# Down-projection weight sums of a fast matrix product moved to a DRAM scratch, twelve fast blocks for ten, and the first loads reordered

## The chip, the cores and the metric

The kernel runs on one core of a Trainium2 chip. Five engines work side by side, each on its own list of instructions in order: TensorE (PE, matrix products; PEld is its weight load), VectorE (DVE), ScalarE (ACT), GpSimd (POOL) and SyncE (SP). Transfers are issued by SP, ACT or POOL and carried out by 16 DMA engines. What counts is the device time of one execution in microseconds (us). The kernel before takes 942.4 us, the median of three runs between 942.28 and 942.5.

## The reference

Two layers of a decoder over 256 tokens of 1024 features, all in float32:

```python
for l in range(DEPTH):                       # 2
    u = rms_norm(h, norm_mix_pre[l])
    proj = u @ w_in[l]                       # q, k, v, xr, yr, pp, gates
    attn_br = sliding_window_attention(q, k, v, sinks) @ w_attn_br[l]
    hr = rg_lru(causal_depthwise_conv(xr, ...), ...)
    rnn_br = (hr * gelu(yr)) @ w_rnn_br[l]
    pool_br = multi_scale_pool(pp, ...) @ w_pool_br[l]
    merged = g0 * attn_br + g1 * rnn_br + g2 * pool_br      # g = sigmoid(gates)
    h = h + rms_norm(merged @ w_out[l], norm_mix_post[l])
    m = rms_norm(h, norm_mlp_pre[l])
    y = square(relu(m @ w_mlp_up[l])) @ w_mlp_down[l]       # 1024 -> 4096 -> 1024
    h = h + rms_norm(y, norm_mlp_post[l])
```

## The kernel before, in words

**Weights.** Every weight matrix is cut into units of 128 x 1024 floats (512 KB). A unit is loaded by SP into one of seven buffers `raw` (`load_to`, L163), split into a high and a low part by ACT (L95) and DVE (L96) (`split_to`; eight buffers `wh`, eight `wl`), and used by TensorE. A full product takes three matmuls, high x high, high x low, low x high (`mm3`, L103 to L105). A load waits until DVE has split the unit that held its buffer seven loads earlier. `take(n)` hands out the next n units and splits as far as needed; `ahead` splits two more.

**A layer** runs in stages: key/value and query projections (12 units); the branch stage, a list `ORDER` of 26 steps (`pp0 gp0 pp1 ... br1`, 74 units), with the attention's parts spread between them; the output projection (8 units); the MLP. Steps with `pp`, `yr`, `xr` take a pair of units (`w_unit2`, L336 and L338) and end in `joined` (L344, L345); steps with `g` are gates (`gate`, L743) and steps with `b` projections (`project`), four units each.

**The MLP.** The 4096 hidden features are 16 blocks of 256. `up(j)` makes block j (two units, 48 matmuls of 256 columns). Ten blocks (`nstr = NBLK - PLAIN`) then go through a Strassen product: `down(j)` makes seven products of three matmuls of 512 columns, 21 in all. The last six (`PLAIN`) go through `plain`: two halves of the block, two of the tokens, two of the columns, three matmuls each, 24 in all. `UPS` says how many `up` run in the step of each Strassen block. The seven products need the block's two down units in four forms `w1` to `w4`. `w1` is the first unit and `w4` half of the second. `w2` and `w3` are sums of quarters of the two: `dma_sums` makes the 1024 columns of `w2` for two blocks at a time with POOL transfers into SBUF, a plain load (L870) and an adding one (L872); `weight_sums` adds the two halves of `w3` on DVE (L887, L888); `weight_forms` splits both. After the Strassen blocks `drain` combines four of the products on DVE while the plain blocks run; the last three plain blocks (`LAST`) are done token tile by token tile.

**The start.** `x` comes in two tiles of 128 tokens: the first half of tile 0 first, its second half between the two halves of weight unit 0, tile 1 after unit 1. `first_features` transposes a quarter of `x` on TensorE (L245) and writes it scaled as high and low part (L249, L250). `warm_up` (L136) runs idle matmuls between. `KV_ORDER` is the order in which the four units of the first projection meet the two token tiles.

**Order.** A scheduler puts each engine's instructions in order at build time; POOL and SP carry them out one after the other, each waiting for what it needs. POOL does, before the change, the small zero fills of `joined`'s buffers (L604, L702) and the twenty loading and adding transfers of each layer's sums.

Of the kernel before, what the change touches and what calls it, by code (L numbers as in the profile page):

```python
# [26 lines left out]
WARM = (6, 2, 2)  # L27
# [4 lines left out]
X1_AT = 2  # L32
# [6 lines left out]
PLAIN = 6  # L39
LAST = 3  # L40

UPS = (2, 1, 1, 2, 1, 1, 2, 1, 1, 1)
NBLK = 16
SQRT_2_PI = 0.7978845608028654
# [9 lines left out]
KV_ORDER = ((0, 0), (1, 0), (0, 1), (1, 1), (2, 0), (2, 1), (3, 0), (3, 1))  # L54
KV_MID = 1
# [8 lines left out]
def trunk(ctx, tc, x, wts, rgw, par, gpost, eye, ctab, out):  # L64
# [11 lines left out]
    psum = ctx.enter_context(tc.tile_pool(name="psum", bufs=8, space=PSUM))  # L76

# [56 lines left out]
    def warm_up(n):  # L134
        for i in range(n):
# [3 lines left out]
    NHU = wts.shape[0]  # L139
    st = {"load": 0, "split": 0, "use": 0}  # L140
    raw_t, hu_t = {}, {}

    nstr = NBLK - PLAIN
    pair_at = [[(l + 1) * (NHU // L) - 64 + 6 + 2 * j + 2 * (sum(UPS[:j - 1]) + 1 if j else 0) for j in range(nstr)]
               for l in range(L)]
    half = {i + 1 for at in pair_at for i in at}

    per_layer = NHU // L
    fine = {i + l * per_layer for l in range(L) for i in [*range(FINE[0]), *range(per_layer - 64, per_layer - 64 + FINE[1])]}

    def load_to(n):
        while st["load"] < min(n, NHU):
            i = st["load"]
            r = raws.tile([P, HU_COLS], F32, tag="raw", name=f"raw{i}")
            if i == 0:
                for k in range(2):
                    nc.sync.dma_start(r[:, 512 * k:512 * k + 512], wts[i][:, 512 * k:512 * k + 512])
                    if k == 0:
                        nc.sync.dma_start(h[:, 0, 512:1024], x[0:P, 512:1024])
            elif i in half:  # L160
                nc.sync.dma_start(r[:, 512:1024], wts[i][:, 512:1024])
            else:
                nc.sync.dma_start(r[:], wts[i])  # L163
            raw_t[i] = r
            st["load"] += 1

    def split_to(n):
        while st["split"] < min(n, NHU):
# [3 lines left out]
            wh = his.tile([P, HU_COLS], F32R, tag="wh", name=f"wh{i}")  # L172
            wl = los.tile([P, HU_COLS], F32R, tag="wl", name=f"wl{i}")
            parts = 2 if i in fine else 1
            for k in range(parts):
                sl = slice(k * HU_COLS // parts, (k + 1) * HU_COLS // parts)
                split(wh[:, sl], wl[:, sl], r[:, sl])
# [10 lines left out]
    def ahead():  # L188
        split_to(st["use"] + AHEAD)
# [152 lines left out]
    def joined(o, pss, first):  # L342
        for n, ps in enumerate(pss):
# [78 lines left out]
    load_to(X1_AT)  # L422
    nc.sync.dma_start(h[:, 1, :], x[P:T, :])
    fa, fb = first_features(0, 0), first_features(0, 1)
# [4 lines left out]
    next(fb)  # L429
    warm_up(WARM[2])  # L430
    next(fb)
    split_to(2)
# [3 lines left out]
    for l in range(L):  # L436
# [14 lines left out]
        def kv_first():  # L451

            pss = [bank([P, 512]) for _ in range(2)]
            for n, (i, tt) in enumerate(KV_ORDER):
# [4 lines left out]
                if n == KV_MID:  # L459
                    for part in range(2):  # L460
                        for _ in hp(first_features)(1, part):
                            pass
# [105 lines left out]
        if l == 0:  # L568
# [3 lines left out]
            hq = take(4)  # L572
            q0 = [qkv_part(1, tt, hq) for tt in range(2)]
# [25 lines left out]
        def unit_pp(j):  # L599
# [4 lines left out]
            nc.gpsimd.memset(xp[:, :, 0:16], 0.0)  # L604
# [88 lines left out]
        def unit_xr(j):  # L693
            rg = ttile([P, 2, 2, P], nm="rg")
            nc.sync.dma_start(rg[:], rgw[l, j])
# [6 lines left out]
            nc.gpsimd.memset(xp[:, :, 0:3], 0.0)  # L702
# [37 lines left out]
        def gate(br, nh):  # L740
            for tt, ps in enumerate(t_unit(uh, ul, nh)):
                th = ttile([P, 512], nm="th")
                A.activation(th[:], ps[:], AF.Tanh, scale=0.5 if l else nrm[:, tt, 2:3])  # L743
                ths[br, nh, tt] = th
            ahead()
# [15 lines left out]
        for nm in ORDER:  # L761
            kind, j = nm[0:2], int(nm[2])
            if nm == "pg0":
# [46 lines left out]
        prods, t8s = {}, {}  # L810
# [28 lines left out]
        def up(j):  # L839
            ps = w_unit(take(2), uh, ul)  # L840
# [23 lines left out]
        def dma_sums(j0):  # L864


# [281 lines left out]
```

## Time and profile before

| | us |
|---|---|
| median of 3 runs | 942.4 |
| profiled execution | 942.54 |
| its span, first to last instruction | 940.8 |
| PE busy / DVE / ACT / POOL | 932.4 / 757.2 / 631.8 / 37.7 |
| DMA bytes | 188.98 MB, mean 201 GB/s |
| of these issued by POOL | 20.97 MB |

"Busy" of PE counts a matmul from its start to its modelled end, so matmuls that follow each other closely overlap, and the spacing of the starts is what a matmul costs. The chain of waits goes back from the last instruction, each time to what released it. The DMA share of a stretch is the mean busy time of the 16 DMA engines; it counts the time that packets took, waiting for memory included. In layer 0 the branch stage lies between 44 and 272 us and the MLP between 290 and 460; in layer 1 some 463 us later.

### The profile page before, as it was taken

Reading aid. Unit: us, or ns where it says so; the run is one execution under the profiler, and the core shown is the slowest. Engines: PE = TensorE matmul, PEld = TensorE weight load, DVE = VectorE, ACT = ScalarE, POOL = GpSimd, SP = SyncE. Lnnn points to the kernel's source line nnn. Section 1 sums busy time; section 2 is a strip of 40 time slices with the busy share of each in tenths; the row PEclk is TensorE's granted clock in tenths of the full one; section 3 lists DMA queues with packets and bytes.
Section 4 is the critical chain, followed back from the end, with each engine's and each line's share of the span. In section 5 each row is a group of like instructions: output and inputs, shape, how many; then the busy total and the mean of one; then the engine's idle time right before and its main releaser. Section 6 shows DMA issues by size and latency. Waiting matters only on the chain.

```text
span 940.8 us, 14349 instructions
## 1 busy us (share of the span) xinstructions
PE 932.4 (99%) x5196; PEld 801.2 (85%) x5196; DVE 757.2 (80%) x1365; ACT 631.8 (67%) x1092; POOL 37.7 (4%) x60
## 2 busy tenths in 40 slices
PE   9999999999999999999999999999999999999997
PEld 6888987888888999998888888888888889999986
DVE  6878997889868887988586788786898598888964
ACT  7765765689637786767475666656896468767741
POOL 0000000000011111100000000000000110110000
PEclk9999999999999999999999999999999999999999
DMA  8855454643867888957457545545438688987631
GB/s 333 289 198 163 152 188 137 218 150 117 283 208 200 254 245 264 271 169 253 134 190 258 170 148 178 179 141 189 161 109 299 176 266 233 264 255 236 219 95 45
DMA packets 57351, 188.98 MB, mean 201 GB/s; under 512 B 6080, under 2 KB 6720, under 8 KB 57280
## 3 DMA queue, kind: packets, MB, share of 16 engines
q1 hardware_dynamic: 48528, 166.79, 53.0%
q0 software_dynamic: 8320, 20.97, 9.9%
q8 instruction: 41, 0.67, 0.3%
q10 hardware_dynamic: 432, 0.30, 0.1%
q14 instruction: 30, 0.25, 0.1%
HBM read 186.99 MB, written 1.05 MB: 200 GB/s over the span
## 4 chain that ended last, share of the span: by engine, by line
PE 99%; DMA 0%; DVE 0%; ACT 0%; SPq 0%; DVEq 0%; issue 0%
PE ps L103 18%; PE ps L104 18%; PE ps L105 18%; PE ps L336 9%; PE ps L376 8%; PE pr L103 6%; PE pr L104 6%; PE pr L105 6%; PE ps L338 5%; PE ps L507 1%; PE ps L555 1%; PE ps L544 1%; PE ps L259 1%; PE ps L487 0%; DMA h<-x 0%; PE ps L736 0%
## 5 line engine op out<-in xcount | busy, mean ns | idle before, releaser
L96 DVE TENSOR_TENSOR wl<-raw,wh 128x1024 fp32r<-128x1024 f32 (+1 forms) x304 | 334.2, 1123 | 69.2 <-ACT wh L95 60.8
L95 ACT ACTIVATE wh<-raw 128x1024 fp32r<-128x1024 f32 (+1 forms) x304 | 288.3, 983 | 138.7 <-PE ps L105 52.8
L103 PE MATMUL ps<-m,wh 128*128 128x256 f32 x448 | 126.8, 283 | 0.0
L105 PE MATMUL ps<-m,wl 128*128 128x256 f32 x448 | 126.8, 283 | 0.0
L104 PE MATMUL ps<-m,wh 128*128 128x256 f32 x448 | 126.7, 283 | 0.0
L336 PE MATMUL ps<-u,wh 128*128 128x512 f32 x384 | 96.9, 394 | 0.0
L103 PEld LDWEIGHTS ps<-m,wh 128*128 128x128 f32 x448 | 85.9, 192 | 1.0
L104 PEld LDWEIGHTS ps<-m,wh 128*128 128x128 f32 x448 | 85.9, 192 | 1.0
L105 PEld LDWEIGHTS ps<-m,wl 128*128 128x128 f32 x448 | 85.9, 192 | 0.0
L103 PE MATMUL ps<-wh,u 128*128 128x512 f32 x208 | 82.4, 396 | 0.0
L104 PE MATMUL ps<-wl,u 128*128 128x512 f32 x208 | 81.6, 392 | 0.0
L105 PE MATMUL ps<-wh,u 128*128 128x512 f32 x208 | 81.1, 392 | 0.0
L336 PEld LDWEIGHTS ps<-u,wh 128*128 128x128 f32 x384 | 69.4, 189 | 13.6 <-issue 0.7
L338 PEld LDWEIGHTS ps<-u,wl 128*128 128x128 f32 x384 | 52.4, 190 | 3.8
L338 PE MATMUL ps<-u,wl 128*128 128x256 f32 x384 | 53.5, 282 | 0.0
L103 PEld LDWEIGHTS ps<-wh,u 128*128 128x128 f32 x208 | 39.4, 190 | 9.0 <-issue 0.7
L105 PEld LDWEIGHTS ps<-wh,u 128*128 128x128 f32 x208 | 39.3, 189 | 8.4
L104 PEld LDWEIGHTS ps<-wl,u 128*128 128x128 f32 x208 | 39.3, 189 | 7.8 <-DVE wl L96 0.3
L526 ACT ACTIVATE pr<-ps,s 128x128 f32<-128x128 f32 (+1 forms) x64 | 25.9, 430 | 20.1 <-DVE s L517 15.7
L376 PE MATMUL ps<-wh,u 128*128 128x512 f32 x160 | 38.6, 392 | 0.0
L104 PE MATMUL pr<-wl,hid 128*128 128x512 f32 (+1 forms) x102 | 38.5, 378 | 0.0
L103 PE MATMUL pr<-wh,hid 128*128 128x512 f32 (+1 forms) x102 | 38.4, 377 | 0.0
(262 smaller groups left out, 1996.5 us busy)
## 6 DMA issues: line engine op xcount, KB each, us to landing
raw<-wts SPq DMA_DIRECT2D x295, 512.0 KB, 4.5
dsum<-wts POOLq DMA_DIRECT2D x40, 512.0 KB, 6.6
raw<-wts SPq DMA_DIRECT2D x22, 256.0 KB, 4.6
gB<-gpost SPq DMA_DIRECT2D x4, 512.0 KB, 7.5
rg<-rgw SPq DMA_DIRECT2D x8, 256.0 KB, 4.2
out<-h SPq DMA_DIRECT2D x3, 256.0 KB, 2.0
h<-x SPq DMA_DIRECT2D x2, 256.0 KB, 3.7
h<-x SPq DMA_DIRECT2D x1, 512.0 KB, 6.5
```

Of the source, the lines that this page charges most:

```text
L95: A.activation(hi, src, AF.Copy)
L96: V.tensor_tensor(out=lo, in0=src, in1=hi.bitcast(F32), op=ALU.subtract)
L103: PE.matmul(o, lh, rh, start=start, stop=False, **kw)
L104: PE.matmul(o, lh, rl, start=False, stop=False, **kw)
L105: PE.matmul(o, ll, rh, start=False, stop=stop, **kw)
L259: PE.transpose(banks[c // 4][:, c % 4, :], src[c // 4][:, (c % 4) * P:(c % 4 + 1) * P], ident)
L336: PE.matmul(ps[:], ws[0][c], x2[:, :, c, :], start=c == 0, stop=False)
L338: PE.matmul(ps[:, 0, :], ws[1][c], x2[:, 0, c, :], start=False, stop=c == 7)
L376: PE.matmul(o, xx[:, c, tsl], ww[c], start=(n == 0 and c == 0), stop=(n == 2 and c == 7))
L507: PE.matmul(sc[hd // hp][:, hd % hp, :], qT[a, j // 2][rows, j % 2, blk * P:(blk + 1) * P], kTs[0][rows, a, 0:w], start=True, stop=True)
L526: A.activation(pr[:, j, :], sc[i][:, j, :], AF.Exp, bias=negm[:, hd:hd + 1], accum_out=sums[:, hd:hd + 1])
L544: PE.transpose(ps[:, g, :], g8["p"](4 * b + g)[:, kt * P:(kt + 1) * P], ident)
```

## The change

The four forms of a Strassen block's weights are now all loaded as stream units. `w1` and `w4` come from a new input `dnw` that holds the pairs; `w2` and `w3` come from a scratch tensor in DRAM, one of 1 MB for each block and layer, which transfers alone fill during the branch stage. For the twelve steps 2, 4, ... 24 of `ORDER` one block is made, in six transfers:

1. POOL writes a few bytes of a tile that the branch stage has just made (`mark`) into the scratch. What fills the scratch must wait for this.
2. SP copies two times 512 KB from `dnw` into the scratch, DRAM to DRAM.
3. POOL issues three adding transfers one after the other, DRAM to DRAM: 512 KB, 256 KB, 256 KB; each needs what was there before.

`PLAIN` goes from 6 to 4, so twelve blocks of a layer are Strassen blocks and four are plain. `dma_sums`, `weight_sums` and `weight_forms` go. The zero fills go from POOL to DVE. The recurrence's small weights `rg` are loaded two steps of `ORDER` ahead. At the start `x` is loaded in quarters among the first weight units, the key/value projection takes both token tiles of a unit before the next unit, and the first query projection follows unit by unit in the same way (`q_first`).

```diff
-WARM = (6, 2, 2)
+WARM = (6, 3)
+X_AFTER = {0: ((1, 0),), 1: ((0, 1), (1, 1))}
-PLAIN = 6
+PLAIN = 4
-UPS = (2, 1, 1, 2, 1, 1, 2, 1, 1, 1)
+UPS = (2, 1, 1, 1, 1, 1, 1, 1, 1, 1, 1, 1)
+BATCH, SUM_AT = 1, tuple(range(2, 26, 2))
-KV_ORDER = ((0, 0), (1, 0), (0, 1), (1, 1), (2, 0), (2, 1), (3, 0), (3, 1))
+KV_ORDER = ((0, 0), (0, 1), (1, 0), (1, 1), (2, 0), (2, 1), (3, 0), (3, 1))
...
+    def sums_copy(l, j0):
+        t = sums[l, j0]
+        nc.gpsimd.dma_start(t[:, :, 0, 0:1].rearrange("b i n -> (b i) n"), mark["t"])
+        for k in range(BATCH):
+            nc.sync.dma_start(t[k, 0], dnw[l, j0 + k, 0])
+            nc.sync.dma_start(t[k, 1].rearrange("p (b n) -> p b n", b=2),
+                              dnw[l, j0 + k, :, :, 512:1024].rearrange("b p n -> p b n"))
+    def sums_add(l, j0, step):
+        t = sums[l, j0]
+        for k in range(BATCH):
+            if step == 0:
+                dst = t[k, 0].rearrange("p (b n) -> p b n", b=2)
+                src = dnw[l, j0 + k, 1, :, 0:512].unsqueeze(1).to_broadcast([P, 2, 512])
+            elif step == 1:
+                dst, src = t[k, 1, :, 0:512], t[k, 0, :, 0:512]
+            else:
+                dst, src = t[k, 1, :, 512:1024], t[k, 1, :, 0:512]
+            nc.gpsimd.dma_start(dst, src, accum_op=ALU.add)
...
+        def pair(j):
+            stream.extend([(dnw[l, j, 0], HU_COLS), (dnw[l, j, 1, :, 512:1024], 512)])
+        def sum_units(j):
+            stream.extend((sums[l, j // BATCH * BATCH][j % BATCH, i], HU_COLS) for i in range(2))
...
+        def q_first():
+            pss = [bank([P, 512]) for _ in range(2)]
+            for i in range(4):
+                hu, = take(1)
+                for tt in range(2):
+                    s_hu(pss[tt][:], hu, uh, ul, 2 * i, tt, i == 0, i == 3)
+                ahead()
+            return [qkv_out(1, tt, pss[tt]) for tt in range(2)]
...
-            nc.gpsimd.memset(xp[:, :, 0:16], 0.0)
+            V.memset(xp[:, :, 0:16], 0.0)
...
-        for nm in ORDER:
+        rgs_raw = {}
+        for k, nm in enumerate(ORDER):
             kind, j = nm[0:2], int(nm[2])
+            for nm2 in ORDER[k:k + 3]:
+                if nm2[0:2] == "xr" and int(nm2[2]) not in rgs_raw:
+                    rgs_raw[int(nm2[2])] = rg = ttile([P, 2, 2, P], nm="rg")
+                    nc.sync.dma_start(rg[:], rgw[l, int(nm2[2])])
+            if k in SUM_AT:
+                j0 = BATCH * SUM_AT.index(k)
+                sums_copy(l, j0)
+                for step in range(3):
+                    sums_add(l, j0, step)
...
-        def dma_sums(j0):
-            t = acts.tile([P, 2, 2, 512], F32, tag="lo", name="dsum")
-            for j in js:
-                nc.gpsimd.dma_start(t[:, j - j0], wts[pair_at[l][j]].rearrange("p (b n) -> p b n", b=2))
-            for j in js:
-                nc.gpsimd.dma_start(t[:, j - j0], wts[pair_at[l][j] + 1][:, 0:512].unsqueeze(1).to_broadcast([P, 2, 512]),
-                                    accum_op=ALU.add)
...
-            V.tensor_tensor(out=t34[:, 0, :], in0=t12[:, 0, :], in1=r0[:, 512:1024], op=ALU.add)
-            V.tensor_tensor(out=t34[:, 1, :], in0=t34[:, 0, :], in1=r1[:, 512:1024], op=ALU.add)
```

The names of the scratch tensors in the lists below are `sums0_9` for block 9 of layer 0; a load `raw78` is the stream unit with number 78, counted from 0. What the change moves in the lists of instructions, at the three places of which the prediction speaks:

SP's list in the branch stage of layer 0, around the load of unit 78, the first of the projection `br0`; before:

```order
L163 DMA raw76_2461<-wts 128x1024 [waits DVE_49]
L163 DMA raw77_2525<-wts 128x1024 [waits DMAHW1_49,DVE_49]
L163 DMA raw78_2545<-wts 128x1024 [waits DMAHW2_49,DVE_49,Activation_49]
L163 DMA raw79_2563<-wts 128x1024 [waits DMAHW3_49,DVE_49,Activation_49]
L163 DMA raw80_2581<-wts 128x1024 [waits DMAHW4_49,DMAHW5_49,DVE_49,Activation_49]
```

and with the change:

```order
L215 DMA raw76_2547<-wts 128x1024 [waits DMAHW3_49,DVE_49,Activation_49]
L215 DMA raw77_2611<-wts 128x1024 [waits DMAHW4_49,DVE_49]
L155 DMA sums0_9_115<-dnw 16x8192 [waits DMAHW5_49,DMASW4_49]
L156 DMA sums0_9_115<-dnw 256x1x512 [waits DMAHW6_49]
L155 DMA sums0_10_116<-dnw 16x8192 [waits DMAHW7_49,DMASW5_49]
L156 DMA sums0_10_116<-dnw 256x1x512 [waits DMAHW0_49]
L215 DMA raw78_2637<-wts 128x1024 [waits DMAHW1_49,DVE_49,Activation_49]
L215 DMA raw79_2655<-wts 128x1024 [waits DMAHW2_49,DVE_49,Activation_49]
```

Four copies into the scratch now stand between the loads of units 77 and 78, and the first of each pair waits for one of POOL's transfers (DMASW), the mark of its block.

POOL's list before, from the branch stage of layer 0 to the first sums of the MLP:

```order
L604 MEMSET xp 128x2x16 x4
L702 MEMSET xr 128x2x3 x4
L870 DMA dsum<-wts 128x1024 x2
L872 DMA dsum<-wts 128x2x512 x2
L870 DMA dsum<-wts 128x1024 x2
```

and with the change, from the marks of blocks 9 and 10 to that of block 11:

```order
L153 DMA sums0_9_115<-xr_2349 2x1 [waits DVE_49]
L153 DMA sums0_10_116<-xr_2349 2x1
L169 DMA sums0_9_115<-dnw 256x1x512 [waits DMAHW5_49,DMASW4_49]
L169 DMA sums0_10_116<-dnw 256x1x512 [waits DMAHW7_49,DMASW7_49,DMASW5_49]
L169 DMA sums0_9_115<-sums0_9_115 128x512 [waits DMAHW6_49,DMASW6_49]
L169 DMA sums0_10_116<-sums0_10_116 128x512 [waits DMAHW0_49,DMASW7_49]
L169 DMA sums0_9_115<-sums0_9_115 128x512 [waits DMASW0_49]
L169 DMA sums0_10_116<-sums0_10_116 128x512 [waits DMASW3_49,DMASW1_49]
L153 DMA sums0_11_117<-th_2767 2x1 [waits Activation_49]
```

POOL's list is now one chain of marks and adds; the mark of a later block stands behind all adds of the block before it. Blocks 3 and 4, 5 and 6, 9 and 10 go in pairs, the other six alone.

PE's list at the start, from the last warm-up matmul behind the first four transposes of `x`; before:

```order
L136 MATMUL ps<-idt,warm 128x256
L245 MATMUL ps<-idt,h 128x128 x4
L136 LDWEIGHTS warm
L136 MATMUL ps<-idt,warm 128x256
L136 LDWEIGHTS warm
L136 MATMUL ps<-idt,warm 128x256
L103 MATMUL ps<-wh_128,u 128x512
L104 MATMUL ps<-wl_129,u 128x512
L105 MATMUL ps<-wh_128,u 128x512
```

and with the change:

```order
L139 MATMUL ps<-idt,warm 128x256
L106 MATMUL ps<-wh_156,u 128x512
L107 MATMUL ps<-wl_157,u 128x512
L304 MATMUL ps<-idt,h 128x128 x4
L108 MATMUL ps<-wh_156,u 128x512
L106 MATMUL ps<-wh_156,u 128x512
```

Two matmuls of the first projection now stand ahead of the second set of transposes, which is that of token tile 1 and no longer the second half of tile 0.

More of the change, by code (lines that the diff above doesn't have):

```diff
@@ L140, in trunk @@
     st = {"load": 0, "split": 0, "use": 0}
     raw_t, hu_t = {}, {}
[L143 to L149, printed above, removed]
+    stream, fine = [], set()
+    n_w = iter(range(wts.shape[0]))
```

138 lines of the change are left out of this document (64 added, 74 removed).

## The prediction

> **What bounds the kernel now.** First the page: busy time, the slices, the chain of waits.
>
> ```profile
> PE 932.4 (99%) x5196; PEld 801.2 (85%) x5196; DVE 757.2 (80%) x1365; ACT 631.8 (67%) x1092; POOL 37.7 (4%) x60
> PE   9999999999999999999999999999999999999997
> PE 99%; DMA 0%; DVE 0%; ACT 0%; SPq 0%; DVEq 0%; issue 0%
> ```
>
> The chain that ends last is TensorE from end to end. Since busy hides gaps between pipelined matmuls, I looked at stretches: branch stage and MLP of layer 0, branch stage of layer 1, a stretch in which DVE never rests, and one of 512-column matmuls alone.
>
> ```profile
> 40.00:250.00 210.00, 210.00 (x1124) 175.79 (x1123) 180.03 (x348) 148.44 (x274) 0.66 (x6) 1.00 0.52 172
> 290.00:420.00 130.00, 130.00 (x863) 119.76 (x862) 112.87 (x179) 95.24 (x151) 14.20 (x16) 1.00 0.82 242
> 520.00:690.00 170.00, 170.00 (x918) 142.06 (x918) 138.32 (x276) 116.22 (x219) 0.54 (x5) 1.00 0.48 158
> 220.00:240.00 20.00, 20.00 (x96) 16.76 (x95) 20.00 (x32) 18.11 (x30) 0.00 (x0) 1.00 0.39 132
> 900.00:920.00 20.00, 20.00 (x89) 16.54 (x89) 12.51 (x14) 7.19 (x8) 0.00 (x0) 1.00 0.11 39
> ```
>
> Columns: length, busy time of PE, PEld, DVE, ACT, POOL (instructions), clock, DMA share, GB/s. The last row prices a 512-column matmul: 20.00 / 89 = 0.225 us from start to start, and the chain has 0.23. PE has no hole to fill, so only two things can shorten this kernel: fewer matmuls, and an earlier start. DMA is half idle in the branch stage (0.52, 0.48) and not in the MLP (0.82): that is where the change takes its room.
>
> **The change part by part.**
>
> *Matmuls.* A Strassen block has 21, a plain one 24. Two blocks more in each of two layers: 4 x 3 = 12 fewer, 12 x 0.227 = 2.7 us. They stand on the path, and nothing can hide that gain but a wait.
>
> *The start.* The chain there:
>
> ```profile
> 1.65 4.36 DMA h<-x
> 6.05 1.12 PE ps L245 x4
> 7.17 0.43 PE ps L136 x2
> 7.60 0.43 PE ps L103
> ...
> 9.73 0.31 PE ps L105
> 10.04 0.23 PE ps L103
> ```
>
> Before, the second half of tile 0, third transfer of SP, lands at 6.01, eight transposes are over at 7.17, and matmuls step by 0.43 until about 9.8, then by 0.23: the granted clock doubles there. After, two matmuls need only the first quarter of `x` and the first half unit:
>
> ```profile
> 4.72 0.63 ACT L95 ACTIVATE wh<-raw 128x512 fp32r<-128x512 f32 x1 [1.56 <-DMA raw<-wts]
> 5.39 0.69 DVE L96 TENSOR_TENSOR wl<-raw,wh 128x512 fp32r<-128x512 f32 x1 [0.29 <-ACT wh L95]
> ```
>
> Low part ready at 6.08, so they run at about 5.9 and 6.3. PE's list then holds the transposes of tile 1. Its quarter is SP's fourth transfer, 0.7 behind the third (256 KB), so 6.7; 1.12 for four transposes, and the third matmul starts at 7.9. Until 9.8 that makes 2 + 4 or 5 matmuls against six before: 0.3 us won. Bounds: if the clock comes earlier, since PE rests less, six steps at 0.2 less, 1.2 won; if the fourth transfer and the features behind it come 1 us later, 1.0 lost. I take 0.3. The Trainium skill (TensorE: Matmul & The Clock Gate, Part 1) has the clock released by a free-running window of about 3.4 us of activity: by that rule the moment depends on the phase of the window as much as on the order of work, and the term would be anywhere between 0.3 and 1.2. The step at 9.8 agrees with such a window; one run cannot show its phase.
>
> *DVE, ACT.* The two adds of each of ten blocks go:
>
> ```profile
> L887 DVE TENSOR_TENSOR t<-dsum,raw 128x512 f32<-128x512 f32 x20 | 13.8, 688 | 0.3
> L888 DVE TENSOR_TENSOR t<-t,raw 128x512 f32<-128x512 f32 x20 | 13.7, 686 | 0.0
> L96 DVE TENSOR_TENSOR wl<-raw,wh 128x1024 fp32r<-128x1024 f32 x248 | 297.7, 1222 | 64.9 <-ACT wh L95 56.6 <-PE ps L376 5.7 <-PE ps L338 1.4
> ```
>
> That is 13.7 us of DVE a layer; two more Strassen blocks cost some 3 us each in splits and forms. DVE has 17 of 130 us free in the MLP, and PE does not wait for it there: worth nothing in time. The zero fills on DVE are 16 of some 0.1 us.
>
> *The scratch.* Here lies the risk. Not one transfer from DRAM to DRAM stands in the trace. The nearest rows are the old sums, load and add, 512 KB each, into SBUF, and a store into DRAM:
>
> ```profile
> L872 POOL DMA_DIRECT2D dsum<-wts x20: 1197/1210/1238, 279.9 to 852.8; - x20
> ...
> DMA to landing us min/median/max: 6.3/7.4/9.0
> ```
>
> ```profile
> L870 POOL DMA_DIRECT2D dsum<-wts x20: 557/567/707, 273.8 to 839.6; - x20
> ...
> DMA to landing us min/median/max: 3.9/5.7/9.0
> ```
>
> ```profile
> out<-h SPq DMA_DIRECT2D x3, 256.0 KB, 2.0
> 286.57 1.21 POOL L872 DMA_DIRECT2D dsum<-wts  x1 [5.48 <-issue]
> ```
>
> One block on POOL: mark 0.57 + 2.0 = 2.6; copy, at the price of a load, 3.9 to 5.7; first add 6.3 to 7.4; second add of half the size, an estimate from the same rows (2.0 + half of the rest), 4.2 to 4.7; issue of the third 1.2; then the next mark. Together 18.2 to 21.6. The last row shows the second of two adds issued only after the first had landed, without any wait that the profile names, so a pair of blocks pays both first adds: 3.2 + 3.9 + 2 x 6.3 + 4.2 + 1.2 = 25.1 to 29.6.
>
> Who waits: SP stands before the copy until the mark has landed, and behind the copy stand the weight loads. The tightest place is unit 78, behind the copies of blocks 9 and 10. The rows:
>
> ```profile
> 69.26 1.24 ACT L743 ACTIVATE th<-ps,nrm 128x512 f32<-128x512 f32 x2
> 71.20 0.33 SPq L163 DMA_DIRECT2D raw<-wts  x1
> 225.05 0.33 SPq L163 DMA_DIRECT2D raw<-wts  x1
> 243.13 3.51 DVE L96 TENSOR_TENSOR wl<-raw,wh 128x1024 fp32r<-128x1024 f32 x3
> 250.64 0.39 PE L103 MATMUL ps<-wh,rnh 128*128 128x512 f32 x1
> ```
>
> The first mark reads the gate that is ready at 70.5, so it lands at 73; SP has issued unit 34 at 71.2 and takes the first copy then. From there five single blocks and two pairs pass until the marks of 9 and 10 land: 5 x 18.2 + 2 x 25.1 = 141 to 5 x 21.6 + 2 x 29.6 = 167, so at 214 to 240. Unit 78 was issued at 225 before, split at 243 and used at 250.6. Split by ACT and DVE takes 2.3, so it must be in SBUF at 248.3. Behind four copies of 512 KB it lands later than usual:
>
> ```profile
> raw<-wts SPq DMA_DIRECT2D x67, 512.0 KB, 4.3
> ```
>
> 4.3 (branch stage) + 4 x 1.25 (512 KB at the 400 GB/s or so at which such transfers follow each other) = 9.3; so SP must issue it by 239, and the chain may take 239 - 1 - 73 = 165. In the middle of the two sums, 154, PE waits for nothing; at the medians, 167, it waits some 3 us in each layer. I take the middle: the rows come from an MLP with a DMA share of 0.82, the branch stage has 0.52, but the scratch adds to that. Per block it moves 1.05 MB of copies and 1.05 MB of adds. From the MLP's queues:
>
> ```profile
> q1 hardware_dynamic: 6920, 22.58, 51.8%
> q0 software_dynamic: 3497, 8.70, 30.1%
> ```
>
> q1 moves 22.58 MB in 67 us of all engines, 0.335 MB/us; q0 takes 39 us, of which half its bytes at that rate are 13 and the adds 26, 0.167 MB/us. A block is 3.1 + 6.3 = 9.4 us; twelve, 113 of some 200 us. With 0.52 that is over 1; these rates hold waiting too, so it can fit, barely. If a block lands late after all, all loads of the MLP are still far away (its first sums are read near 294): what counts is SP alone.
>
> *The sums read back* replace 1 MB of POOL's transfers a block in the MLP by 1 MB of plain loads, without the adds: the share of 0.82 goes down. Nothing on the path.
>
> Sum against the profiled 942.54: - 2.7 - 0.3 = 939.5; against the median 942.4 it is 939.4. I forecast 939.5.
>
> **The rivals.**
>
> *The chain on POOL is longer than the branch stage: slower.* From 165 us on, each us more is a us of waiting in each layer. Speaking for it: DRAM at both ends is the heavier case, and the share over 1. Against it: 154 lies below, and once SP stands still no loads compete with the adds. At the medians 939.5 + 2 x 3 = 945.5; with 175, 960; with every step at its dearest row (9.0, 9.0, 5.5; 27.3 and 37), 210 and some 1030. The Trainium skill (DMA: Bandwidth & Descriptors, Latency and other measured facts) gives copies between two HBM tensors 207 to 214 GB/s in each direction. By that figure the first copy of a block moves in 2.5 us and not 1.25 (an estimate), about 9 us over the chain: 163, still at the edge. No run so far shows it.
>
> *The gain is lost at the end of the MLP: the same.* Between the last Strassen block and the last three plain ones stood three plain blocks (72 matmuls, 16.3 us); now one stands there (5.4). In its time and that of the last Strassen product (4.8), DVE has to split eight units (9.8) and do `drain` and the hidden parts (eight operations of 0.69, 5.5): 15.3 against 10.2, unless the scheduler has it split earlier into the eight buffers. Five buffers are free or freed before, so I expect it hidden; if half is not, 1.5 us in each layer, 942.5.
>
> *More at the start: faster by 1.2 instead of 0.3*, 938.6.
>
> **How the numbers follow.** Forecast 939.5 (own range 939.0 to 940.4): 0.47. More at the start: 0.10, also faster. The gain lost: 0.13. The chain too long: 0.30, of which half lies above 950. A measurement of this kernel tells 0.2%, 1.9 us, from no change. Faster 0.57, same 0.13, slower 0.30. Range 938.0 to 960: below it 0.05, above it 0.13.
>
> **What would show it.** Right: PE dense in all stages, twelve matmuls fewer, SP's waits for POOL's marks below 15 us each, DMA share in the branch stage 0.9 or more and in the MLP below 0.8. Wrong: PE idle before `br0`, with ACT or DVE waiting for a DMA, and adds that land in over 8 us; then the sum of the chain is the step that failed. If PE waits just before the last three blocks, the second rival; if the third matmul starts after 8.5, the start.

## The result, and the profile after

The changed kernel takes **1021.8 us** (median, 1021.4 to 1023.7) against 942.45 us for the kernel before beside it: ratio **1.0846, 95% interval [1.0832, 1.0859]**. It is 79 us slower. The forecast was 939.5 us with a range up to 960, so it was wrong in sign and far outside the range; the rival "the chain on POOL is longer than the branch stage" is the case that came.

The page of the changed kernel: span, busy time, and the chain that ended last, by engine.

```profile
span 1021.7 us, 14624 instructions
PE 957.6 (94%) x5183; PEld 815.7 (80%) x5183; DVE 748.4 (73%) x1373; ACT 641.2 (63%) x1110; POOL 78.7 (8%) x100
PE 53%; DMA 30%; issue 12%; POOL 2%; SPq 1%; DVE 1%; ACT 1%; POOLq 0%; DVEq 0%; ACTq 0%
```

TensorE held 99% of the chain before; now it holds 53%, and DMA, which held nothing, holds 30%. The stages by windows (columns as in the prediction: busy time of PE, PEld, DVE, ACT, POOL, then clock, DMA share, GB/s):

```profile
40.00:140.00 100.00, 100.00 (x570) 84.58 (x569) 86.06 (x210) 64.81 (x137) 9.02 (x11) 1.00 0.72 217
140.00:250.00 110.00, 90.43 (x431) 73.01 (x430) 62.12 (x114) 54.67 (x97) 18.78 (x23) 0.91 0.81 227
250.00:340.00 90.00, 82.42 (x354) 66.83 (x353) 65.69 (x97) 57.26 (x90) 11.41 (x14) 0.94 0.86 262
340.00:420.00 80.00, 80.00 (x532) 73.72 (x531) 65.13 (x104) 58.68 (x95) 0.00 (x0) 1.00 0.79 265
```

TensorE is dense until 140 us, has holes from there to the end of POOL's work at about 336, and is dense in the MLP. That is layer 0; in layer 1 the holes lie in the same part, between 600 and 800 us. The loss lies in the branch stage, from its middle on, and the clock is below 1 in just those rows. The chain of waits in the undisturbed part just ahead of the first hole shows what one block of sums costs on POOL (start, length, what):

```profile
114.35 4.60 DMA sums<-xp
...
118.97 4.22 DMA sums<-dnw
...
123.90 10.85 DMA sums<-dnw
...
135.14 0.83 POOL sums L169
135.96 4.17 issue
...
140.15 0.52 POOL sums L169
140.67 3.71 DMA sums<-yr
```

Mark 4.6, copy 4.9 with its issue, first add 11.2, second add 5.0, issue of the third 0.5: 26.3 us from mark to mark, where the prediction had 18.2 to 21.6. That the first add is not dear by chance is seen in the list of DMA issues (count, KB each, median us to landing):

```profile
sums<-dnw SPq DMA_DIRECT2D x48, 512.0 KB, 5.3
sums<-dnw POOLq DMA_DIRECT2D x24, 512.0 KB, 10.8
sums<-sums POOLq DMA_DIRECT2D x48, 256.0 KB, 4.6
```

Who waits, from the table of waits (us in total, times, longest), first of the engines, then of SyncE's queue:

```profile
POOL sums L169 <- DMA sums<-dnw: 297.6, 35, 11.3
ACT wh L98 <- DMA raw<-wts: 114.8, 32, 17.2
```

```profile
SPq L155 <- DMA sums<-xr: 77.2, 4, 21.0
SPq L155 <- DMA sums<-yr: 74.9, 4, 21.0
SPq L155 <- DMA sums<-th: 61.5, 6, 20.1
SPq L155 <- DMA sums<-xp: 46.0, 4, 17.4
```

POOL waits for its first adds; SyncE stands at the copies (L155) for 260 us until a mark has landed; ScalarE then waits for weights that SyncE issued late. How that reaches TensorE is seen on ScalarE's own timeline at the first hole (start, length, instruction, in brackets the idle time ahead of it):

```profile
157.33 1.06 ACT L98 ACTIVATE wh<-raw 128x1024 fp32r<-128x1024 f32 x1 [17.18 <-DMA raw<-wts]
158.81 1.06 ACT L609 ACTIVATE pT<-ps 128x512 f32<-128x512 f32 x2
```

ScalarE works in order. It stood 17 us at the split of a unit that TensorE did not need yet, and behind that split stood the attention's evictions (`pT`), which TensorE did need. The late load hurt here when its split came up in ScalarE's list, before TensorE came to multiply by the unit. SyncE issued that load, the first of six, at 146.9 us, right behind four copies into the scratch:

```profile
146.93 4.35 SPq L215 DMA_DIRECT2D raw<-wts  x6
```

It landed about 10.4 us later, when ScalarE's wait ended; the prediction had 9.3 for a load behind four copies. Of the 17 us some 7 were thus waiting for the issue, and the rest was the landing in a crowd of transfers that had been held back together.

### The profile page after: what moved, and what is told of

Read it like the earlier page. It is cut to its first block, busy times and chain, and to the rows that moved or that the text cites. A ratio compares the mean times of both kernels' runs of the same rounds, so it can differ in the third digit from the quotient of the medians.

```text
span 1021.7 us, 14624 instructions
## 1 busy us (share of the span) xinstructions
PE 957.6 (94%) x5183; PEld 815.7 (80%) x5183; DVE 748.4 (73%) x1373; ACT 641.2 (63%) x1110; POOL 78.7 (8%) x100
## 3 DMA queue, kind: packets, MB, share of 16 engines
q1 hardware_dynamic: 62880, 216.08, 60.7%
q0 software_dynamic: 14208, 25.17, 15.4%
## 4 chain that ended last, share of the span: by engine, by line
PE 53%; DMA 30%; issue 12%; POOL 2%; SPq 1%; DVE 1%; ACT 1%; POOLq 0%; DVEq 0%; ACTq 0%
DMA sums<-dnw 17%; PE ps L108 9%; PE ps L107 9%; PE ps L106 9%; PE ps L436 6%; DMA sums<-sums 5%; PE pr L106 5%; PE pr L107 5%; PE pr L108 5%; DMA sums<-th 2%; POOL sums L169 2%; DMA raw<-wts 2%; DMA sums<-yr 2%; PE ps L395 1%; DMA sums<-xr 1%
## 5 line engine op out<-in xcount | busy, mean ns | idle before, releaser
L98 ACT ACTIVATE wh<-raw 128x1024 fp32r<-128x1024 f32 (+1 forms) x370 | 355.9, 993 | 246.8 <-DMA raw<-wts 114.8
L99 DVE TENSOR_TENSOR wl<-raw,wh 128x1024 fp32r<-128x1024 f32 (+1 forms) x370 | 412.2, 1135 | 122.6 <-ACT wh L98 114.9
L395 PE MATMUL ps<-u,wh 128*128 128x512 f32 x384 | 100.7, 405 | 11.2 <-ACT pT L609 11.2
L107 PE MATMUL ps<-wl,u 128*128 128x512 f32 x224 | 90.1, 402 | 5.7 <-DVE wl L99 5.7
L106 PE MATMUL ps<-wh,u 128*128 128x512 f32 x224 | 90.6, 405 | 5.1 <-ACT pr L589 3.2
L108 PE MATMUL ps<-wh,u 128*128 128x512 f32 x224 | 90.0, 402 | 0.0
L169 POOL DMA_DIRECT2D sums<-sums x48 | 42.6, 888 | 241.7 <-DMA sums<-dnw 165.0
L106 PEld LDWEIGHTS ps<-wh,u 128*128 128x128 f32 x224 | 43.7, 195 | 15.9 <-ACT pr L589 3.6
L107 PE MATMUL pr<-wl,xf 128*128 128x512 f32 x144 | 56.4, 392 | 0.0
L106 PE MATMUL pr<-wh,xf 128*128 128x512 f32 x144 | 56.4, 392 | 0.0
L108 PE MATMUL pr<-wh,xf 128*128 128x512 f32 x144 | 56.0, 389 | 0.0
L107 PEld LDWEIGHTS ps<-wl,u 128*128 128x128 f32 x224 | 43.7, 195 | 14.9 <-DVE wl L99 6.2
L108 PEld LDWEIGHTS ps<-wh,u 128*128 128x128 f32 x224 | 43.6, 195 | 9.2
## 6 DMA issues: line engine op xcount, KB each, us to landing
sums<-dnw POOLq DMA_DIRECT2D x24, 512.0 KB, 10.8
```

The costliest lines, as they stand in the source:

```text
L98: A.activation(hi, src, AF.Copy)
L99: V.tensor_tensor(out=lo, in0=src, in1=hi.bitcast(F32), op=ALU.subtract)
L106: PE.matmul(o, lh, rh, start=start, stop=False, **kw)
L107: PE.matmul(o, lh, rl, start=False, stop=False, **kw)
L108: PE.matmul(o, ll, rh, start=False, stop=stop, **kw)
L169: nc.gpsimd.dma_start(dst, src, accum_op=ALU.add)
```

## The experiments

Every ratio is to the kernel before, run on the same chip beside it. Theory 1: POOL's chain of adds is longer than the branch stage, and the branch stage is tied to it, so it runs at POOL's pace. Theory 2: the scratch's bytes fill the DMA engines, and the weights come late whoever waits for whom.

### Everything but the scratch

```
-            stream.extend((sums[l, j // BATCH * BATCH][j % BATCH, i], HU_COLS) for i in range(2))
+            stream.extend((dnw[l, j, i], HU_COLS) for i in range(2))
...
-                sums_copy(l, j0)
-                for step in range(3):
-                    sums_add(l, j0, step)
```

> The changed kernel without marks, copies and adds; the forms w2 and w3 are loaded from the pair's own two units, so the down-projection's result is wrong, with the same loads, splits and matmuls. If the whole loss comes from the scratch, the rest of the change is left: 942.5 - 2.7 (twelve matmuls) + 2.2 (the start, by the trace of the changed kernel) = 942.0, between 941.5 and 942.5. If the end of the MLP with one plain block costs something, 943.5 or more, with PE idle just before the last three blocks.

Measured: 939.95 us, ratio 0.9971 [0.9959, 0.9984]. Its page, to be held against the changed kernel's:

```profile
span 938.2 us, 14350 instructions
PE 928.6 (99%) x5183; PEld 798.7 (85%) x5183; DVE 747.9 (80%) x1373; ACT 643.3 (69%) x1110; POOL 0.2 (0%) x4
```

Fewer matmuls, the new start, the splits and the end of the MLP are together worth 2.5 us, close to the 3.0 of the prediction's sum. The time lies below the expected 941.5 to 942.5: the 2.2 us that the expectation counted as lost at the start were not. The end of the MLP costs nothing: TensorE has no hole ahead of the last three blocks. The scratch alone makes the loss, and the two pages divide it: span minus busy time is 64.1 us after and 9.6 here, so 54.5 us more are idle; the same 5183 matmuls take 957.6 against 928.6, so 29.0 us are matmuls at a lower clock. Together 83.5, the difference of the spans. The Trainium skill (TensorE: Matmul & The Clock Gate, HAM oscillation) says that a TensorE which waits for transfers longer than its window falls back to half clock and starts the next work cold; this trace agrees, with 0.91 and 0.94 in the windows that have holes and 1.00 in the others.

### Marks and copies without the adds

```
                 sums_copy(l, j0)
-                for step in range(3):
-                    sums_add(l, j0, step)
```

> The changed kernel without the adding transfers; the marks and the copies stay where they were, so w2 and w3 hold unsummed quarters and the result is wrong. Theory 1: POOL has only marks to do, each is issued when its tile is ready, SP stands 4 us at most, 942 to 944. Theory 2: the copies are 25 of 38 MB of the scratch's payload; if bytes alone decide, part of the loss stays, 955 to 990.

Measured: 938.45 us, ratio 0.9957 [0.9942, 0.9971]. All copies, all marks and all reads of the scratch are there, and TensorE is dense. So the adds are what costs. (The time is below the 942 to 944 of theory 1, which counted the same 2.2 us as lost at the start; and the copies are 25 of the 50 MB that the scratch takes in, not of 38.) This run also shows at what times the branch stage would come to its marks if nothing held it (POOL's timeline; marks of blocks 3 and 4, 5 and 6, 9 and 10), and below it stand the same marks in the changed kernel:

```profile
120.13 1.03 POOL L153 DMA_DIRECT2D sums<-yr  x2 [18.78 <-DVE yr L717]
144.31 1.03 POOL L153 DMA_DIRECT2D sums<-yr  x2 [23.16 <-DVE yr L717]
210.93 1.03 POOL L153 DMA_DIRECT2D sums<-xr  x2 [19.90 <-DVE xr L407]
```

```profile
140.67 1.37 POOL L153 DMA_DIRECT2D sums<-yr  x2
179.45 1.36 POOL L153 DMA_DIRECT2D sums<-yr  x2
265.49 1.33 POOL L153 DMA_DIRECT2D sums<-xr  x2
```

Without adds POOL waits for the branch stage at every mark (the brackets); with them it waits in layer 0 at none after the first, and is late by 21, 35 and 55 us. The lateness grows from mark to mark, and the first hole opens already behind the marks of blocks 3 and 4, long before blocks 9 and 10.

### Copies taken from SyncE's queue

```
-            nc.sync.dma_start(t[k, 0], dnw[l, j0 + k, 0])
-            nc.sync.dma_start(t[k, 1].rearrange(...
+            nc.gpsimd.dma_start(t[k, 0], dnw[l, j0 + k, 0])
+            nc.gpsimd.dma_start(t[k, 1].rearrange(...
```

> One edit: the two copies of a block are issued by POOL instead of SP, so that no weight load stands behind a mark any more; bytes, adds and marks are as in the changed kernel. Theory 1 (SP stands behind POOL's chain and the loads come late): PE's waits go nearly all, 942 to 946. Theory 2 (the DMA engines are full, whoever issues): loads still land late and PE waits, 980 or more. What is left between the two would be the tiles that a late mark holds.

Measured: 1022.85 us, ratio 1.0861 [1.0824, 1.0898]: no gain at all, though no load stands behind a mark any more. The theory that SyncE's queue is the one tie falls here. The waits name another, and the window shows what it does:

```profile
ACT ti L740 <- DMA sums<-xr: 83.2, 2, 43.0
PE ps L106 <- ACT ti L740: 57.9, 2, 30.3
```

```profile
220.00:240.00 20.00, 0.00 (x0) 0.00 (x0) 0.00 (x0) 0.00 (x0) 4.67 (x7) 0.60 0.55 111
```

ScalarE's write of `ti` waits 43 us for the mark that reads `xr`. The mark is a transfer out of the tile `xr`, issued when POOL comes to it; until then that tile's buffer cannot be given to the next tile, here `ti`. TensorE stands still for 30 us in one piece instead of in many. So I formed theory 1 anew: two ties, each enough by itself.

### Only the held tile freed

The mark is written from a two-element copy in a small tile that is never reused; SyncE keeps the copies.

```
...
+        m = marks.tile([2 * BATCH, 1], F32, tag="m", name="mk")
+        V.tensor_scalar(m[:], mark["t"], 1.0, None, op0=ALU.mult)
-        nc.gpsimd.dma_start(t[:, :, 0, 0:1].rearrange("b i n -> (b i) n"), mark["t"])
+        nc.gpsimd.dma_start(t[:, :, 0, 0:1].rearrange("b i n -> (b i) n"), m[:])
```

> The changed kernel, but each mark is written from a two-element copy that VectorE makes in a small tile of its own (24 of them, never reused), so that no tile of the branch stage stays held until POOL comes to its mark. SyncE still issues the copies, and still stands at them until the mark has landed. Theory 1 (the branch stage runs at the pace of POOL's chain because SyncE stands behind the marks): nothing that matters is gone, SyncE waits some 250 us for the marks, 1000 to 1022 us. Theory 1b (it is tied by the held tiles): SyncE's waits are covered by the seven raw buffers, 940 to 950 us. Theory 2 (the adds fill the DMA engines, whoever waits): 1015 to 1025 us, with raw loads landing in 6 us and more and little waiting of SyncE for marks.

Measured: 1028.84 us, ratio 1.0917 [1.0899, 1.0935]; 4 us above the highest that any of the three gave, and clearly not theory 1b. SyncE's queue in this run:

```profile
SPq L158 <- DMA sums<-mk: 283.6, 19, 20.8
```

### Both ties cut

Both edits together: the same marks, copies, adds and bytes, in the same order on POOL.

> As the run before it, and the copies are issued by POOL too: SyncE waits for no mark and no tile of the branch stage is held. The same marks, copies and adds, the same bytes. Theory 1 (POOL's chain is longer than the branch stage, and harms only through the two ties): POOL's chain takes 250 to 290 us in each layer as before and ends some 60 to 90 us after the branch stage, TensorE stays dense, 938.5 to 942 us. Theory 2 (the adds fill the DMA engines): raw loads still come late, 1000 us or more. If each holds in part: 945 to 990 us.

Measured: 944.46 us (941.0 to 951.4 over twelve executions), ratio 1.0025 [1.0007, 1.0042]. The four runs make a square: both ties 1021.8, held tiles alone 1022.9, SyncE alone 1028.8, neither 944.5. Either tie costs all, and cutting both gives back 77 us. Theory 2 falls by the same run; its window of the stage that lost most:

```profile
140.00:250.00 110.00, 110.00 (x552) 91.18 (x551) 96.75 (x168) 85.74 (x141) 23.44 (x31) 1.00 0.94 282
```

The DMA share is 0.94, more than the 0.81 of the changed kernel, and TensorE has no hole. Full DMA engines did not hold it up; waiting did, and waiting left the DMA engines emptier.

It is still not the 938.5 to 942 that theory 1 gave. The last add of layer 0 is issued at 360.8 us, long after the branch stage, and in the chain at the second MLP's start a weight load needs 7.35 us, where the two loads from `wts` issued there in the run without the scratch land in 4.0:

```profile
360.78 0.82 POOL L172 DMA_DIRECT2D sums<-sums  x1 [7.61 <-DMA sums<-sums]
```

```profile
756.75 7.35 DMA raw<-wts
```

So theory 3: what remains is POOL's chain running on beside the first loads of the MLP, where TensorE has less in store.

### One mark per layer

The copies on POOL, and only the first block of each layer with a mark.

```
-        nc.gpsimd.dma_start(t[:, :, 0, 0:1].rearrange("b i n -> (b i) n"), mark["t"])
+        if j0 == 0:
+            nc.gpsimd.dma_start(t[:, :, 0, 0:1].rearrange("b i n -> (b i) n"), mark["t"])
...
```

> The changed kernel with the copies issued by POOL and with the mark of the first block of each layer alone; the other eleven blocks wait for nothing but POOL's own queue. Same copies and adds. Theory 1: no tie is left but at the first block, 938.5 to 942 us; a block takes some 20 us, a layer's chain 230 to 250 us and begins at 72 us. Theory 2: 1000 us or more, since the chain now runs without a pause and crowds the loads more, not less.

Measured: 959.06 us, ratio 1.0175 [1.0157, 1.0193]: a miss for both theories. I had not foreseen that blocks without a mark are put at the head of POOL's list, ahead of the first block: the copies begin at 1.26 us and not at 72, and the unmarked blocks of layer 1 follow at once: POOL issues the last add of these 22 blocks at 403.6 us and then stands idle until layer 1's one mark at 551.

```profile
0.00:60.00 60.00, 49.32 (x197) 36.45 (x198) 36.71 (x107) 36.12 (x66) 15.05 (x23) 0.91 1.01 337
60.00:300.00 240.00, 240.00 (x1262) 200.66 (x1261) 197.98 (x376) 160.72 (x292) 55.28 (x70) 1.00 0.99 302
300.00:420.00 120.00, 114.97 (x731) 102.40 (x730) 90.94 (x149) 84.11 (x140) 22.03 (x28) 1.00 1.03 329
```

The run says more than planned. In the middle row the DMA share is 0.99 for 240 us and TensorE is dense; at the start and in the MLP's first part the same traffic comes with 10.7 and 5.0 us of idle TensorE. Of the idle time at the start, some 2 to 3 us are there in the other runs too (1.8 in the first 40 us of the kernel before, 3.3 without the scratch). So bytes of the scratch can cost time (theory 2 in part). My reading, which no run here tests by itself, is that they do so where the loads have no lead yet, at the start and at the first part of the MLP; the marks keep POOL away from the start.

### Without the first add

```
-                for step in range(3):
+                for step in range(1, 3):
```

> The changed kernel without the first add of each block (the one of 512 KB); the second and third stay, so the sums that the MLP reads are incomplete and the result is wrong by that. Theory 1 (the length of POOL's chain decides): a block is mark 3.7, copy 5.3, issue 1.2 and add 4.6, or 15 us in place of 25, twelve of them with two pairs about 150 to 175 us per layer, near the length of the branch stage: 938.5 to 950 us. Theory 2 (bytes of the adds on the DMA engines): half of them are gone, so about half of the loss, 975 to 985 us.

Measured: 940.18 us, ratio 0.9970 [0.9958, 0.9981]. Both ties are in place and harmless. The marks in POOL's timeline (blocks 3 and 4, 5 and 6, and 8):

```profile
122.21 1.08 POOL L153 DMA_DIRECT2D sums<-yr  x2 [0.59 <-DVE yr L717]
153.56 1.34 POOL L153 DMA_DIRECT2D sums<-yr  x2
201.52 0.82 POOL L153 DMA_DIRECT2D sums<-xr  x1
```

Late by 2, 9 and 11 us against the run without adds (block 8 stands at 190.51 there), and TensorE is dense. So 11 us of lateness cost nothing, and the 20.5 us of the changed kernel at blocks 3 and 4 cost a hole: the store of loaded and split weights covers something between the two, as far as different marks can be compared.

### The first add in two halves

```
-                dst = t[k, 0].rearrange("p (b n) -> p b n", b=2)
-                src = dnw[l, j0 + k, 1, :, 0:512].unsqueeze(1).to_broadcast([P, 2, 512])
+                for b in range(2):
+                    nc.gpsimd.dma_start(t[k, 0, :, 512 * b:512 * b + 512], dnw[l, j0 + k, 1, :, 0:512], accum_op=ALU.add)
+                continue
```

> The changed kernel with the first add of a block issued as two adds of 256 KB, one per half, in place of one of 512 KB; ties, marks, copies and bytes as they are. If the price of the first add (10.8 us in the changed kernel, against 6.3 to 7.4 in the prediction) is its size: two adds that land together in 5 to 6 us, 5 us less per block, 60 us less for a layer's chain of twelve, and a good part of the loss gone: 955 to 1000 us. If POOL holds the second of the two until the first has landed: 10 us for the two, nothing won, 1010 to 1030 us.

Measured: 1002.88 us, ratio 1.0633 [1.0617, 1.0648], between the two answers. The halves of 256 KB take a median of 9.5 us each when they are issued back to back, while the second and third adds, of the same 256 KB but alone, take 5.8:

```profile
sums<-dnw POOLq DMA_DIRECT2D x48, 256.0 KB, 9.5
sums<-sums POOLq DMA_DIRECT2D x48, 256.0 KB, 5.8
```

Splitting does not make the work cheap; the two share one rate. It wins some 2 us in most single blocks and next to nothing in a pair. From its first mark to its last add POOL's chain takes 254.2 us in layer 0 and 247.1 in layer 1, where the changed kernel has 258.3 and 260.0: 17.0 us less. The spans of the two profiled executions differ by 15.7 (1021.7 and 1006.0), the medians by 19. So here, with the ties in place, a us of POOL's chain was about a us of the kernel.

### Two blocks at once, ties cut; and with the halves

On the run with both ties cut, one mark for two blocks:

```
-BATCH, SUM_AT = 1, tuple(range(2, 26, 2))
+BATCH, SUM_AT = 2, tuple(range(2, 26, 4))
```

> The run with both ties cut (944.46 us), with two blocks taken together: one mark for two blocks, their four copies, then their two first, two second and two third adds, so that the landings of one lie under those of the other; six pairs per layer. Theory 3 (the 4 us that the run with both ties cut still lost come from POOL's chain running on to 368 us, beside the MLP's first loads, where the DMA share is 0.94 to 1.04): a pair takes 35 to 38 us as the two pairs did before, the chain ends by 295 to 310 us, the wait of 2.8 us at the second MLP's start is gone: 938.5 to 941 us. Against it (the loss is the adds' traffic, wherever it lies): 943 us or more.

> As the run with two blocks at once, and each first add as two of 256 KB. Theory 3: a little shorter chain still, 938.5 to 941 us, not to be told from the run with two blocks at once. Against it: 943 us or more.

Two blocks at once: 944.78 us (939.5 to 949.0), ratio 1.0020 [1.0002, 1.0039], no better than with one block at a time, and on the side that speaks against theory 3 as it stood. The chain ends some 50 us earlier, with a last add issued at 308.6, but the first MLP's loads come at about 292, still beside the adds: there too a weight load takes 6.4 us, and 7.0 at the second MLP. With the halves as well: **938.53 us, ratio 0.9963 [0.9951, 0.9975]**, the fastest of the runs that make the sums in full, and faster than the kernel before. Its last adds are issued at 283.8 us in layer 0 and at 742.9 in layer 1, before the MLP's loads at 292.7 and 753.9. Its halves go out every 3 to 4 us, though each still takes a median of 8.4 to land:

```profile
84.34 0.84 POOL L167 DMA_DIRECT2D sums<-dnw  x1 [3.21 <-issue]
88.29 0.81 POOL L167 DMA_DIRECT2D sums<-dnw  x1 [3.11 <-issue]
```

```profile
140.00:250.00 110.00, 110.00 (x552) 91.17 (x552) 95.89 (x163) 84.99 (x140) 28.59 (x39) 1.00 1.00 298
```

The window's DMA share is 1.00, and TensorE is dense. The same bytes cost nothing here, so the loss is not the adds' traffic wherever it lies. The two runs agree with theory 3 as sharpened: the chain has to end before the MLP's first loads, and an end at 308 is no better than one at 361. I had expected 308 to do. The halves change the adds too, and no run moves the end of the chain alone.

### The short chain with both ties kept

The changed kernel with the last two edits alone (two blocks at once, first add in halves).

> The changed kernel with both ties kept (SyncE issues the copies, the marks read tiles of the branch stage), and only POOL's chain made shorter as in the best run: two blocks at once with one mark, each first add as two of 256 KB. If the length of the chain alone decides whether the ties do harm: a pair takes some 34 us where the branch stage comes to the next mark every 38 to 40 us, SyncE waits a few us at each of six marks, 938.5 to 945 us. If the ties harm at any length of the chain: two blocks' copies stand behind each mark, 955 us or more.

Measured: 990.68 us, ratio 1.0518 [1.0499, 1.0538], on the side of the second answer. The expectation took 38 to 40 us between marks, and that is where it failed. The marks of the run without adds lie at 69.6, 100.8, 120.1, 144.3, 190.5 and 210.9 for the blocks that have one here: gaps of 31, 19, 24, 46 and 20, in the mean 28, while a pair here takes 34 to 37 from mark to mark. POOL's third and fourth mark here:

```profile
137.39 0.83 POOL L153 DMA_DIRECT2D sums<-yr  x1
173.28 0.77 POOL L153 DMA_DIRECT2D sums<-yr  x1
```

They are 17 and 29 us late. Behind the third, TensorE stands idle for 7 of the 30 us from 140 on, so 17 us of lateness cost time where 11 did not. SyncE waits up to 26 us at a mark. The shortened chain is still longer than the stage, by 35 us at its last mark in layer 0 (246.3 against 210.9), so the run does not tell the length of the whole chain from its pace at each mark. It shows that with the ties in place this much shortening is not enough, while the run before, with both ties cut, lost nothing.

### The start by itself

The kernel before with the new order of the first transfers, warm-up and first units, and nothing else:

```
-WARM = (6, 2, 2)
+WARM = (6, 3)
+X_AFTER = {0: ((1, 0),), 1: ((0, 1), (1, 1))}
...
-KV_ORDER = ((0, 0), (1, 0), (0, 1), (1, 1), (2, 0), (2, 1), (3, 0), (3, 1))
-KV_MID = 1
+KV_ORDER = ((0, 0), (0, 1), (1, 0), (1, 1), (2, 0), (2, 1), (3, 0), (3, 1))
```

> The kernel before with the new start alone: x in quarters among the first units, the new order of the key and value projection, the first query projection unit by unit, three warm-up matmuls. The prediction said 0.3 us won (942.1). By the trace of the changed kernel, in which the fourth transfer landed at 7.8 and the clock rose only at about 14 us, 2.2 us lost: 944.6.

Measured: 941.52 us (940.9 to 943.3), ratio 0.9994 [0.9985, 1.0004]. It cannot be told from no change, and a term of 0.3 us could not have been. The 944.6 that the changed kernel's trace suggested is refuted.

## Why the prediction was wrong, step by step

- **What bounds the kernel, and matmuls.** Right. TensorE without a hole was the bound, and everything but the scratch gained 2.5 us (predicted 2.7 + 0.3).
- **The start.** Its parts came otherwise. In the changed kernel's chain the fourth transfer lands at 7.79, not 6.7, and matmuls step by 0.43 until past 14 us, not 9.8:

```profile
2.13 5.66 DMA h<-x
7.84 1.12 PE ps L304 x4
...
14.49 0.23 PE ps L106
```

  That is one execution. In the trace of the run without adds, which starts with the same code, they step by 0.23 from 8.2 us on. Other runs with this start lie between (11.0 without the scratch, 11.9 without the first add). So the moment is not set by the order of work alone, and no single trace prices this term. The doubling of the clock that the prediction reads from the steps is seen in the clock row in the run without the scratch (0.53 between 8 and 11 us, 1.00 after); in the traces before and after that row stands at 1.00 throughout.

  Alone, the new start makes no difference that can be told; the other start, "more at the start", is not shown either.
- **DVE and ACT, the end of the MLP.** Right, and the second rival is refuted: no hole there in the run without the scratch.
- **The sum of the chain: the first step that failed.** The prediction had 141 to 167 us from the first mark's landing to that of blocks 9 and 10, and took 154. Measured: the marks go out at 72.71 and 265.49, so 193 us. The term most mis-sized is the first add, 10.85 us (median 10.8) in place of 6.3 to 7.4; then the mark, 4.6 in place of 2.6. The copy, 4.2, was right, and so was the second of a pair's first adds going out only behind the first (38.8 us a pair, against 25.1 to 29.6, for the dearer adds).
- **The tightest place: the second step that failed.** I asked only whether unit 78 would come in time behind blocks 9 and 10, and let the chain have 165 us there. The cover was counted up to TensorE's use of the unit, but ScalarE stands at its split earlier, with attention's evictions behind it. I allowed some 25 us of lateness at that mark (landed by 238, against 213 where the stage wants it: issued at 210.9, landed about 2 later); 11 us were free, and 17 and 20.5 at earlier marks were not. So the first hole opened long before unit 78. By the prediction's own prices the middle of its sums would have been 14 us late there (landed at 227), and 13 us late at blocks 5 and 6: landed at 73 + 3 x 18.2 + 25.1 = 153 to 73 + 3 x 21.6 + 29.6 = 167, against about 147 where the stage wants them (issued at 144.3, landed some 3 later). That lies between what is free and what is not. The forecast of no wait had less room than it claimed, even at those prices.
- **"What counts is SP alone": wrong.** A second tie, the tile that a late mark keeps, holds the branch stage just as fast. The prediction counted who is queued behind a waiting instruction, but not what a waiting transfer holds.
- **The rival that came.** Its mechanism, POOL's chain longer than the stage and each us of it paid, is shown. At the medians its own sum is nearer 943.5 than 945.5 (167 against 165 is 2 us in each layer, not 3). Its price rule gives 939.5 + 2 x (196.5 - 165) = 1002.5 with the measured chain (193, and 3.7 for the landing); measured were 1021.8. The rule would fit with an allowance of 155 us in place of 165; whether that is the smaller cover or the slower matmuls after each wait, no run separates. It had a chance of 0.30, and the range, up to 960, reached only its mild end.
- **The share of the DMA engines.** The rates were near (0.335 and 0.167 MB/us; here 216.08 MB in 60.7% of 1021.7 us is 0.348, and 25.17 MB in 15.4% is 0.160), and "over 1, yet it can fit, barely" came true: in the fastest run the share is 1.00 with TensorE dense. That this was the worry that could be borne, and the latency of a serial chain the one that could not, is the lesson of the case.
- **The signs to look for.** TensorE idle, ScalarE and VectorE waiting for a transfer, adds landing in over 8 us: all were seen, and pointed to the right step, though the second tie was found only by an experiment.

**What stays open.** Why an accumulating transfer of 512 KB within DRAM takes 10.8 us was not settled. Two halves back to back share one rate, so it is not the single instruction. Nor is it POOL's queue or the shape of the transfer by itself: in the run with both ties cut, the second copy of a block (L159) is plain, and of the same size, shape and queue as the first add, and it lands in 6.9 us at the median, with the DMA engines fuller than in the changed kernel:

```profile
L159 POOL DMA_DIRECT2D sums<-dnw x24: 687/698/981, 76.7 to 794.0; - x24
...
DMA to landing us min/median/max: 4.6/6.9/11.4
```

What the accumulating itself is waiting for, no run here tells. Why freeing the tile alone came out 7 us slower than the changed kernel was not followed up. The two runs that end their chain in the MLP spread over some 10 us from execution to execution; I do not know why.

## What to carry to other kernels

Cost a serial chain of small transfers by latency, at the dearest near row, and hold it against each point where other work meets it, with the spacing of those points read from a trace and the lateness that the slack there was seen to cover; the share of the DMA engines says little about it. A wait on a slow queue reaches further than the instructions behind it: whatever tile the waiting transfer still has to read stays taken, so give a pacing signal a tile of its own and keep slow transfers off the queue that feeds the weights. Where such work is moved under a quiet stage, see that it ends before the next busy one begins: that was the difference between the two untied runs that lost some 5 us and the one that lost nothing, though the adds differed too.

## What the runs showed of the hardware that I had not expected

- An accumulating transfer from DRAM to DRAM is slow to land: 10.8 us for 512 KB and 4.6 us for 256 KB alone (changed kernel), 9.5 us each for two of 256 KB back to back. Plain copies of 512 KB between the same places took 5.3 from SyncE's queue, and 5.3 and 6.9 (first and second copy of a block, both ties cut) from POOL's. The Trainium skill (DMA: Bandwidth & Descriptors, Anatomy of one DMA) fits a transfer from this path by 2.0 us plus the bytes at 436 GB/s, an estimate of 3.2 us for 512 KB; these runs do not agree with that for accumulating transfers (10.8 us).
- A mark of eight bytes from SBUF to DRAM takes 3.7 us at the median, and 4.6 in the chain above: a transfer used as a signal is not cheap.
- TensorE can stay dense for 240 us at a DMA share of 0.99, and stand idle for 20 of 110 us at a share of 0.81.
- Of the 83.5 us between the spans with and without the scratch, 29.0 were not waiting but matmuls at a lower clock; the clock is below 1 only in the windows with holes (0.91 and 0.94).
